# Five of ten neighbourhood value tiles written into the state-space stretch, and attention's first loads written ahead of the rest

## The chip, the cores and the metric

The kernel runs on one core of a Trainium2 chip. The metric is device microseconds of one launch, the median over runs. The core has a tensor engine (PE, with PEld for its weight loads), a vector engine (DVE), a scalar engine (ACT), GpSimd (POOL) and a sync engine (SP), which here issues every transfer. Each takes its own queue of instructions in order; a wait at the head of a queue holds what stands behind it.

## The reference, cut to what matters

Two layers over 1024 latent tokens and 256 context tokens (1280 in all, ten tiles of 128), model width 1024. In each layer one input projection feeds three groups of heads:

```python
na_q, na_k, na_v, df_q, df_k, df_v, s_z, s_xbc, s_dt = jnp.split(h @ w_in, cuts, axis=-1)
y_na = neighbourhood_attention(rms_norm(na_q), rms_norm(na_k), na_v, kc, vc, na_rpb)   # 4 heads of 64
y_df = diff_mixer(df_q, df_k, df_v, ...)     # differential attention: softmax(m0) - lam * softmax(m1)
y_ssm = ssm_mixer(s_z, s_xbc, s_dt, ...)     # bidirectional state-space scan in chunks of 128 tokens
y = jnp.concatenate([y_na, y_df, y_ssm], axis=-1)      # then output projection, residual, gated MLP
```

The change concerns `na_v = h @ w_in[...]` (256 columns, all ten token tiles) and what stands around it. What is computed stays the same.

## The kernel before

All projections work in pairs of high and low parts: an input block or a weight block is split into a rounded part and a remainder, and three matmuls (high by high, high by low, low by high) take the place of one. `load_w` fetches a 128x1024 weight block, copies its high part on ACT (line 268) and subtracts on POOL (line 269). `proj` does 128 output features for chunks of 512, 512 and 256 tokens, three times eight matmuls for a chunk (`proj_chunk`, lines 422 to 424). `proj_tm` does a tile of 128 tokens by 256 features, also 24 matmuls (lines 446 to 448), with weights of two blocks.

The mixer of a layer runs in this order. First come the state-space inputs and states. Then `dfproj` does the differential queries, keys and values, and `naqk` the neighbourhood queries and keys, four blocks in all. During `dfproj` and `naqk` the state-space output (`ssd_all`, a generator with 40 steps in layer 0 and 32 in layer 1, four to a chunk of 128 tokens) runs in the background: after every chunk or tile of a projection, `bg_step` adds `SR` to an account and takes one step from the generator for each whole unit in it. `bg_finish` takes what is left. The output of a state-space chunk ends with a normalization and two stores (`ydd<-zt` and `ydd<-y`, line 1049). This is called the state-space stretch here.

At the handover the memory pools of the state-space output (`ts`) and of the neighbourhood queries and keys (`np`) close, a pool `nv` with two buffers for value tiles and the pool `da` of differential attention open. Then `proj_tm` does the ten tiles of the neighbourhood values. Each is copied by ACT (`nv`, line 846) and stored to DRAM (`nvd`, line 847). Now `df_stream`, the generator of differential attention, is the background, with one step per tile. Its first step loads the keys of two heads (`load_k`: `ks`, four transfers, line 727) and the queries of one tile (`load_q`: `qst`, four transfers, line 734), and does scores (line 759). Each step is one unit: scores of a head for 128 queries, and transposes and values of the unit before.

When the values are done, the layer's input `h` is released. In its place opens the pool `tn` for neighbourhood attention (`natt`), which loads windows of the values (`vw`, `vx`), keys (`nk`, `nqd`) and queries (`nqs`), and the mixed stretch begins: steps of differential attention, of `natt` and of a modulation stream (`ada_native`) are written in turns by the numbers in `streams`.

What sets the order on each engine: the code is traced once, and each instruction gets a priority by its place in the code. A list scheduler then plays the program through with estimated durations, and gives an engine that is free the earliest written instruction among those that are ready, a tile's memory included. So an instruction written early goes first only if it is ready, and one written later may go ahead of it. Memory of a closed pool is reused tile by tile. Three PSUM buffers (`mm`) serve the projections.

Of the kernel before, what the change touches and what calls it, by code (L numbers as in the profile page):

```python
# [10 lines left out]
F32 = mybir.dt.float32  # L11
# [15 lines left out]
NF = 22  # L27
NBIG = -1e30
EB = 6
SR = 1.2  # L30
PA = 0
OORD = (6, 7, 4, 5, 2, 3, 0, 1)
HX = 6
# [43 lines left out]
B_NAV = 22  # L77
# [3 lines left out]
def hybrid_kernel(ctx, tc, xin, cc, w_ada, bada, gmf, w_in, w_dt, w_out, w_up, w_dn, vec, cst, rope, nab, out):  # L81
    nc = tc.nc
    V, S, G, PE, SP = nc.vector, nc.scalar, nc.gpsimd, nc.tensor, nc.sync
# [58 lines left out]
    def at_prio(gen, off):  # L142
        while True:
            with prio(off):
                if next(gen, "end") == "end":
                    return
            yield

    def phase(name, side="left"):
        return tc.tile_pool(name=name, bufs=1, side=side, reuse_waits="tile")  # L150
# [3 lines left out]
    bg_rate = [1.0]  # L154
    bg_due = [0.0]

    def bg_step():
        bg_due[0] += bg_rate[0]
        while bg_due[0] >= 1.0:
            bg_due[0] -= 1.0  # L160
            next(bg[0], None)

    def bg_finish():
        for _ in bg[0]:
            pass
# [251 lines left out]
    def proj_chunk(wh, wl, c0, n, evac, order=range(KT)):  # L417
        ps = mmt()
        for i, k in enumerate(order):
            ks = slice(k * 128, (k + 1) * 128)  # L420
            r = hsl(hH, k, c0, n)
            PE.matmul(ps[:, :n], wh[:, ks], r, start=(i == 0), stop=False)  # L422
            PE.matmul(ps[:, :n], wh[:, ks], hsl(hL, k, c0, n), start=False, stop=False)  # L423
            PE.matmul(ps[:, :n], wl[:, ks], r, start=False, stop=(i == KT - 1))  # L424
        evac(ps[:, :n], c0, n)
        bg_step()

    def proj(src, chunks, evac, order=range(KT)):
        wh, wl = load_w(src)
# [8 lines left out]
    def proj_tm(src2, tiles, evac):  # L438
        w2 = [load_w(s) for s in src2]
        for t in tiles:  # L440
            ps = mmt()
            for k in range(KT):
                wh, wl = w2[k // 4]
                ks = slice((k % 4) * 256, (k % 4 + 1) * 256)
                th, tl = hsl(hH, k, t * 128, 128), hsl(hL, k, t * 128, 128)
                PE.matmul(ps[:, :256], th, wh[:, ks], start=(k == 0), stop=False)
                PE.matmul(ps[:, :256], th, wl[:, ks], start=False, stop=False)
                PE.matmul(ps[:, :256], tl, wh[:, ks], start=False, stop=(k == KT - 1))
            evac(ps[:, :256], t)
            bg_step()  # L450

    ud = [dr.tile([8, 128, T], F32, name=f"ud{l}") for l in range(NL)]
    zd = [dr.tile([4, 128, T], F32, name=f"zd{l}") for l in range(NL)]
# [2 lines left out]
    nvd = [dr.tile([T, 256], F32, name=f"nvd{l}") for l in range(NL)]  # L456
# [58 lines left out]
    def mixer(l):  # L515
        full = l == 0
        qchunks = ALLC if full else MAINC
        NT = 10
# [149 lines left out]

        sd = ExitStack()
        bg[0] = ssd_all(l, sd.enter_context(phase(f"ts{l}")), dts, lah.bitcast(F32), ecs, full)  # L670
        bg_rate[0] = SR
        dfproj(l, dfv, qchunks, lam, gq, gnq, sub, lam_init)


        npx = ExitStack()
        np_ = npx.enter_context(phase(f"np_{l}", "right"))

# [23 lines left out]

            proj(w_in[l, (B_NAQ, B_NAK)[iq] + b], ALLC if iq else qchunks, ev)

        for b in range(2):
            naqk(1, b)
            naqk(0, b)

        bg_finish()
        sd.close()
        npx.close()  # L710
        nvx = ExitStack()
        nv_p = nvx.enter_context(phase(f"nv_{l}", "right"))

        p = da.enter_context(phase(f"da_{l}"))

        def df_stream():
# [74 lines left out]
            def values(b, qt):  # L791
# [34 lines left out]
                SP.dma_start(out=ydd[l][2 + b, 0, :, c0:c0 + n], in_=oh.bitcast(F32))  # L826
                SP.dma_start(out=ydd[l][2 + b, 1, :, c0:c0 + n], in_=sq)

            for i in range(len(units) + 1):
                if i < len(units):  # L830
                    scores(*units[i])
                if i > 0:
                    b, qt, hh = units[i - 1]
                    turn(b, qt, hh)
                    if hh:
                        values(b, qt)
                yield
# [1 line left out]
        ksp = [None]  # L839
        dfs = at_prio(df_stream(), PD)  # L840
        bg[0] = dfs
        bg_rate[0] = 1.0

        def evn(ps, t):
            nv = nv_p.tile([128, 256], F32, tag="nv", name="nv", bufs=2)
            S.copy(out=nv, in_=ps)
            SP.dma_start(out=nvd[l][t * 128:(t + 1) * 128, :], in_=nv)

        proj_tm([w_in[l, B_NAV], w_in[l, B_NAV + 1]], range(NT), evn)
        bg[0] = iter(())  # L850
        nvx.close()
        close_h()
# [5 lines left out]
        with phase(f"tn{l}", "right") as p2:  # L858
            nu = 40 if full else 32
            ksp[0] = p2  # L860
            streams = [(dfs, nu - NT), (natt(l, p2, full), nu), (at_prio(ada_native(p2, todo), PA), 4 * len(todo))]
            total = max(n for _, n in streams)
            done = [0] * len(streams)
            for i in range(total + 2):
                if i == int(HI * total):
                    for k in range(HX, KT):
                        for e in range(2):
                            SP.dma_start(out=(hH, hL)[e][k][0].bitcast(F32), in_=ydd[l][k, e, :, 0:512])
                for j, (g, n) in enumerate(streams):
                    while done[j] * total <= i * n and done[j] <= n:  # L870
                        done[j] += 1
                        if next(g, "end") == "end":
                            done[j] = n + 1
            for g, _ in streams:
                for _ in g:
                    pass
# [1004 lines left out]
```

## Time and profile before

| | us |
|---|---|
| median of 3 runs | 3579.18 (3574.5 to 3580.07) |
| the profiled execution | 3568.3 |
| its span, first to last instruction | 3566.3 |
| mean granted TensorE clock | 0.967 |

The profiled execution is one run of its own. Its span is the time from the first to the last instruction, and 2 us lie around it. The granted clock is a share of full speed, 2.4 GHz; 0.50 is the lower of its two levels, 1.2 GHz. In tables by stretches a number of microseconds behind an engine is its busy time in that stretch, and the number in brackets counts its instructions.

### The profile page before, as it was taken

The page shows a single profiled execution, that of the slowest core. Times are in us where ns is not written, and L with a number is a line of the kernel's source. Part 1 is how long each engine was busy: PE and PEld are TensorE (multiplying, and loading weights), DVE is VectorE, ACT ScalarE, POOL GpSimd, SP SyncE. Part 2 cuts the span into 40 slices and gives each one's busy share as a digit, 9 for nine tenths or more (in the row PEclk, how much of TensorE's full clock was granted, in tenths as well). Part 3 has the DMA queues.
Part 4 walks back from the last instruction along what each step waited for, and adds up shares of the span by engine and source line. Part 5 has one row for each costly group of instructions (what it writes and reads, how often), then busy time and mean ns, then how long its engine had stood idle before and what let it go on. Part 6 is the DMA issues. An engine that isn't in the chain of part 4 may idle for free. (4 is left out here: it accounts for less than half of the span.)

```text
span 3566.3 us, 50227 instructions
## 1 busy us (share of the span) xinstructions
PE 3274.8 (92%) x17970; PEld 2579.0 (72%) x17970; DVE 2272.8 (64%) x4074; ACT 1514.2 (42%) x2641; POOL 1797.8 (50%) x1391
## 2 busy tenths in 40 slices
PE   7998998899888999998998998998998979999899
PEld 3876776667767887887786876776766757777677
DVE  6635875667485555556768745884674666776753
ACT  4233433778263233333335433344774533333343
POOL 2136663667244444544554226663674455555444
PEclk8999999999999999999999999998999989999999
DMA  8355444753722222225443245447555422222633
GB/s 294 105 189 180 133 124 134 193 153 107 260 90 68 89 91 79 89 86 183 145 133 110 84 145 198 125 131 190 169 172 194 152 71 89 92 93 99 240 114 118
DMA packets 328473, 491.24 MB, mean 138 GB/s; under 512 B 28320, under 2 KB 182048, under 8 KB 327968
## 3 DMA queue, kind: packets, MB, share of 16 engines
q1 hardware_dynamic: 328224, 488.03, 43.0%
q8 instruction: 142, 2.33, 0.3%
q14 instruction: 107, 0.88, 0.1%
HBM read 349.25 MB, written 138.67 MB: 137 GB/s over the span
## 5 line engine op out<-in xcount | busy, mean ns | idle before, releaser
L269 POOL TENSOR_TENSOR wL<-wr,wH 128x1024 fp32r<-128x1024 f32 x80 | 204.3, 2557 | 425.9 <-ACT wH L268 384.9
L1226 POOL TENSOR_TENSOR wL<-wr,wH 128x1024 fp32r<-128x1024 f32 (+1 forms) x102 | 229.5, 2252 | 339.5 <-ACT wH L1223 308.5
L760 DVE TENSOR_SCALAR_CACHE_REDUCE e<-s 128x512 f32<-128x512 f32 (+1 forms) x400 | 229.4, 590 | 140.9 <-PE s L759 135.6
L1226 POOL TENSOR_TENSOR wL<-wd,wH 128x512 fp32r<-128x512 f32 (+1 forms) x134 | 215.2, 1623 | 201.0 <-ACT wH L1223 200.6
L1226 POOL TENSOR_TENSOR wL<-ws,wH 128x512 fp32r<-128x512 f32 x168 | 254.1, 1532 | 111.8 <-ACT wH L1223 111.7
L1226 DVE TENSOR_TENSOR bL<-br,bH 128x512 fp32r<-128x512 f32 x154 | 145.4, 948 | 132.0 <-ACT bH L1223 131.0
L93 ACT ACTIVATE e<-e,nm 128x1280 f32<-128x1280 f32 (+1 forms) x144 | 183.3, 1273 | 41.6 <-DVE nm L763 34.4
L1223 ACT CAST wH<-wr 128x1024 fp32r<-128x1024 f32 (+1 forms) x102 | 91.8, 905 | 252.7 <-PE mm L1218 184.0
L1223 ACT CAST wH<-ws 128x512 fp32r<-128x512 f32 x168 | 98.0, 619 | 232.6 <-PE mm L1218 104.1
L772 POOL TENSOR_TENSOR e<-e 128x1280 f32<-128x1280 f32 (+1 forms) x72 | 193.0, 2682 | 3.9
L759 PE MATMUL s<-ks,qst 128*128 128x512 f32 (+1 forms) x400 | 164.5, 449 | 27.9 <-DMA qst<-qkd 13.9
L995 POOL TENSOR_SCALAR mf<-cs,lah 128x128 fp32r<-128x128 f32 x288 | 138.8, 498 | 51.6 <-PE s L997 50.9
L1373 DVE SCALAR_TENSOR_TENSOR fa<-fpad,vc,fa 128x1282 f32<-128x1282 f32 (+1 forms) x88 | 140.6, 1654 | 36.5 <-ACT fa L93 36.5
L1218 PE MATMUL A<-bL,wH 128*128 128x512 f32 x352 | 141.0, 400 | 12.0 <-DVE bL L1226 11.7
L1223 ACT CAST bH<-br 128x512 fp32r<-128x512 f32 x154 | 95.3, 619 | 125.5 <-DMA br<-hdd 55.6
L1223 ACT CAST wH<-wd 128x512 fp32r<-128x512 f32 (+1 forms) x134 | 86.7, 683 | 139.6 <-PE B L1218 70.3
L422 PE MATMUL mm<-h_0H,wH 128*128 128x512 f32 x320 | 135.0, 423 | 4.4 <-DVE aqs L690 3.1
L1219 PE MATMUL A<-bH,wL 128*128 128x512 f32 x352 | 137.6, 397 | 0.0
L423 PE MATMUL mm<-h_0L,wH 128*128 128x512 f32 x320 | 131.5, 411 | 1.9 <-DVE h_0L L402 1.9
L422 PE MATMUL mm<-h_1H,wH 128*128 128x512 f32 x320 | 131.4, 412 | 1.5 <-ACT z L93 1.5
L424 PE MATMUL mm<-h_1H,wL 128*128 128x512 f32 x320 | 130.3, 407 | 0.0
L424 PE MATMUL mm<-h_0H,wL 128*128 128x512 f32 x320 | 130.0, 406 | 0.0
(871 smaller groups left out, 10652.4 us busy)
## 6 DMA issues: line engine op xcount, KB each, us to landing
wr<-in_w_up_dram SPq DMA_DIRECT2D x94, 512.0 KB
br<-hdd SPq DMA_DIRECT2D x154, 256.0 KB
wa<-in_w_ada_dram SPq DMA_DIRECT2D x56, 512.0 KB
wr<-in_w_in_dram SPq DMA_DIRECT2D x48, 512.0 KB
hdd<-c SPq DMA_DIRECT2D x88, 256.0 KB
wr<-in_w_ada_dram SPq DMA_DIRECT2D x40, 512.0 KB
wd<-in_w_dn_dram SPq DMA_DIRECT2D x38, 512.0 KB
hdd<-fa SPq DMA_DIRECT2D x66, 256.0 KB
```

What stands on the lines that cost most here:

```text
L93: ins = S.activation(**kw)
L269: (eng or G).tensor_tensor(out=wl, in0=wr, in1=wh.bitcast(F32), op=ALU.subtract)
L422: PE.matmul(ps[:, :n], wh[:, ks], r, start=(i == 0), stop=False)
L424: PE.matmul(ps[:, :n], wl[:, ks], r, start=False, stop=(i == KT - 1))
L759: PE.matmul(s_, qst[b, qt][:, mi], ks[b][:, mi, k0 + c:k0 + c + n], start=True, stop=True)
L760: V.tensor_scalar(out=e[:, c:c + n], in0=s_, scalar1=1.0, scalar2=None, op0=ALU.mult, op1=ALU.max, accum_out=mx[:, ci:ci + 1])
L772: G.tensor_tensor(out=es[0][:, 0:nk], in0=es[0][:, 0:nk], in1=es[1][:, 0:nk], op=ALU.add)
L995: (V if hh % 2 else G).tensor_scalar(out=mf[:, hh], in0=C(mk), scalar1=lah[:, e, c, h:h + 1], scalar2=1.0, op0=ALU.mult, op1=ALU.mult)
L1218: PE.matmul(ps, wh, bl, start=False, stop=False, skip_group_check=True)
L1223: S.copy(out=out_h, in_=src)
L1226: le.tensor_tensor(out=out_l, in0=src, in1=out_h.bitcast(F32), op=ALU.subtract)
L1373: V.scalar_tensor_tensor(out=a[:, :W], in0=pads[r][:, j:j + W], scalar=vcol(l, fw + j), in1=a[:, :W], op0=ALU.mult, op1=ALU.add)
```

## The change

The first five value tiles are written between the first and the second block of neighbourhood queries and keys, inside the state-space stretch. The other five stay at the handover, so the value weights are loaded by two calls. The pool `nv` opens before `np`. The background's steps are weighted by the columns of the chunk or tile just done (512 columns are 1, a value tile 0.5), and `SR` is 1.5 in layer 0 and 1.3 in layer 1 instead of 1.2. `df_stream` gets a first step of its own with the keys and two tiles of queries, and it is taken before the value tiles of the handover; scores follow from the third tile on. So 3 instead of 10 of its units are written among the value tiles, and the rest goes into the mixed stretch.

```diff
-SR = 1.2
+SR = (1.5, 1.3)
...
-    def bg_step():
-        bg_due[0] += bg_rate[0]
+    def bg_step(w=1.0):
+        bg_due[0] += bg_rate[0] * w
...
(proj_chunk)
-        bg_step()
+        bg_step(n / 512)
...
(proj_tm)
-            bg_step()
+            bg_step(0.5)
...
-        bg_rate[0] = SR
+        bg_rate[0] = SR[l]
         dfproj(l, dfv, qchunks, lam, gq, gnq, sub, lam_init)
+        nvx = ExitStack()
+        nv_p = nvx.enter_context(phase(f"nv_{l}", "right"))
         npx = ExitStack()
         np_ = npx.enter_context(phase(f"np_{l}", "right"))
...
-        for b in range(2):
-            naqk(1, b)
-            naqk(0, b)
-
+        def evn(ps, t):
+            nv = nv_p.tile([128, 256], F32, tag="nv", name="nv", bufs=2)
+            S.copy(out=nv, in_=ps)
+            SP.dma_start(out=nvd[l][t * 128:(t + 1) * 128, :], in_=nv)
+
+        w_nav = [w_in[l, B_NAV], w_in[l, B_NAV + 1]]
+        naqk(1, 0)
+        proj_tm(w_nav, range(5), evn)
+        naqk(0, 0)
+        naqk(1, 1)
+        naqk(0, 1)
         bg_finish()
         sd.close()
         npx.close()
-        nvx = ExitStack()
-        nv_p = nvx.enter_context(phase(f"nv_{l}", "right"))
...
(df_stream)
+            load_k(0)
+            load_q(0, 0)
+            load_q(0, 1)
+            yield
             for i in range(len(units) + 1):
...
         bg[0] = dfs
-        bg_rate[0] = 1.0
-
-        def evn(ps, t):
-            nv = nv_p.tile([128, 256], F32, tag="nv", name="nv", bufs=2)
-            S.copy(out=nv, in_=ps)
-            SP.dma_start(out=nvd[l][t * 128:(t + 1) * 128, :], in_=nv)
-
-        proj_tm([w_in[l, B_NAV], w_in[l, B_NAV + 1]], range(NT), evn)
+        bg_rate[0] = 2.0
+        bg_due[0] = -2.0
+        next(dfs)
+        proj_tm(w_nav, range(5, NT), evn)
...
-            streams = [(dfs, nu - NT), (natt(l, p2, full), nu), (at_prio(ada_native(p2, todo), PA), 4 * len(todo))]
+            streams = [(dfs, nu - 2), (natt(l, p2, full), nu), (at_prio(ada_native(p2, todo), PA), 4 * len(todo))]
```

## Rows read from the trace of the kernel before

**Rows 1.** The page: busy time, share and instructions of each engine.
```profile
PE 3274.8 (92%) x17970; PEld 2579.0 (72%) x17970; DVE 2272.8 (64%) x4074; ACT 1514.2 (42%) x2641; POOL 1797.8 (50%) x1391
```

**Rows 2.** Table by stretches: length, engines' busy time, clock, DMA share, GB/s.
```profile
487.00:572.00 85.00, 80.15 (x435) 59.32 (x435) 75.97 (x148) 35.75 (x73) 55.96 (x69) 0.96 0.40 123
572.00:590.00 18.00, 11.56 (x83) 10.43 (x82) 9.16 (x20) 6.50 (x16) 4.83 (x5) 0.91 0.55 167
590.00:606.00 16.00, 9.48 (x77) 8.88 (x75) 0.00 (x0) 1.02 (x3) 0.00 (x0) 0.93 1.02 227
606.00:647.00 41.00, 33.01 (x210) 27.01 (x210) 21.56 (x84) 21.70 (x38) 22.89 (x15) 0.87 0.43 114
...
2308.00:2404.00 96.00, 92.86 (x510) 73.24 (x509) 80.67 (x160) 39.80 (x79) 67.73 (x84) 0.98 0.41 127
2404.00:2428.60 24.60, 21.77 (x174) 18.71 (x173) 12.84 (x26) 10.83 (x22) 6.59 (x7) 1.00 0.55 170
2428.60:2445.20 16.60, 12.24 (x106) 12.07 (x105) 0.00 (x0) 0.74 (x2) 0.00 (x0) 0.95 0.92 198
2445.20:2473.40 28.20, 23.17 (x108) 15.70 (x108) 19.57 (x76) 19.18 (x31) 18.15 (x12) 0.73 0.52 144
...
2520.00:2700.00 180.00, 173.95 (x1527) 127.03 (x1526) 125.59 (x521) 137.50 (x276) 127.74 (x94) 0.99 0.52 155
```

**Rows 3.** Timeline of SP's queue: start, duration, line, what, count.
```profile
588.70 0.37 SPq L1049 DMA_DIRECT2D ydd<-y  x1
...
589.81 0.39 SPq L727 DMA_DIRECT2D ks<-qkd  x1
...
606.81 12.24 SPq L847 DMA_DIRECT2D nvd<-nv  x6
...
2426.31 0.37 SPq L1049 DMA_DIRECT2D ydd<-y  x1
2428.24 0.32 SPq L847 DMA_DIRECT2D nvd<-nv  x1
2428.66 2.06 SPq L727 DMA_DIRECT2D ks<-qkd  x4
...
2444.29 3.15 SPq L847 DMA_DIRECT2D nvd<-nv  x4
```

**Rows 4.** Timeline of PE: first scores of differential and of neighbourhood attention.
```profile
606.10 1.19 PE L759 MATMUL s<-ks,qst 128*128 128x512 f32 x2 [6.40 <-DMA qst<-qkd]
...
647.30 0.98 PE L1127 MATMUL ns<-nk,nqs 128*128 128x384 f32 x2 [5.35 <-DMA nk<-nqd]
...
2445.19 1.19 PE L759 MATMUL s<-ks,qst 128*128 128x512 f32 x2 [4.36 <-DMA qst<-qkd]
...
2473.36 0.59 PE L1127 MATMUL ns<-nk,nqs 128*128 128x384 f32 x2 [2.91 <-DMA nk<-nqd]
```

**Rows 5.** Table by stretches, PE's instructions of line 446 alone.
```profile
572.00:590.00 18.00, 7.21 (x23) 0.91 0.55 167
590.00:606.00 16.00, 7.18 (x25) 0.93 1.02 227
606.00:647.00 41.00, 9.76 (x32) 0.87 0.43 114
2404.00:2428.60 24.60, 12.73 (x43) 1.00 0.55 170
2428.60:2445.20 16.60, 9.77 (x35) 0.95 0.92 198
```

**Rows 6.** Timeline of ACT: the first copies of value tiles, layer 0.
```profile
590.10 0.65 ACT L846 COPY nv<-mm 128x256 f32<-128x256 f32 x2 [2.25 <-DMA nqd<-aoh]
```

**Rows 7.** Line 269 in 320 to 590: count, shortest, median and longest, ns.
```profile
L269 POOL TENSOR_TENSOR wL<-wr,wH x8: 2345/2364/2689, 336.1 to 546.5; 128x1024 fp32r<-128x1024 f32 x8
```

**Rows 8.** DMA issues of 2428.6 to 2445.2: count, KB each.
```profile
ks<-qkd SPq DMA_DIRECT2D x4, 640.0 KB
qst<-qkd SPq DMA_DIRECT2D x8, 64.0 KB
```

## Prediction

> **What bounds the kernel now.** I read the page first: PE (the tensor engine) is busy 92% of the span, more than any other engine [rows 1], so the change is worth the PE time that it loses or wins. Next the table by stretches [rows 2], cut at the events that the change touches: the neighbourhood query and key projections (487 to 572 us in layer 0, 2308 to 2404 in layer 1), a drain in which the state-space chain runs out (572 to 590, 2404 to 2428.6), the load of attention's keys (590 to 606, 2428.6 to 2445.2) and differential attention alone (606 to 647, 2445.2 to 2473.4). The reader is to see PE busy and granted clock together. I call a stretch minus busy times clock its lost PE time, since at half clock the same work takes twice as long. Layer 0: 85 - 80.15 x 0.96 = 8.1; 18 - 11.56 x 0.91 = 7.5; 16 - 9.48 x 0.93 = 7.2; 41 - 33.01 x 0.87 = 12.3. Layer 1: 96 - 92.86 x 0.98 = 5.0; 24.6 - 21.77 = 2.8; 16.6 - 12.24 x 0.95 = 5.0; 28.2 - 23.17 x 0.73 = 11.3. The mixed stretch of attention behind them loses little (173.95 busy of 180).
>
> Then SP's queue in order of time [rows 3]: the keys `ks` are issued at 589.81 and 2428.66, 1.1 and 2.4 us after the last state-space output `ydd<-y`. In layer 1 the store of a value tile that stands later in the code than `ks` is ahead of it, at 2428.24: so it is not its place in the code that held `ks` back; it became available when the state-space stretch ended. Last the waits of PE [rows 4]: the first score matmul comes at 606.10 and 2445.19, 16.3 and 16.5 us after `ks`, the first neighbourhood score at 647.30 and 2473.36.
>
> **The change part by part.** *Moved matmuls.* A value tile is 24 matmuls, eight on line 446, which counts tiles [rows 5]: 35/8 = 4.4 tiles stand in the key load of layer 1, where PE is busy 12.24 us with them: 2.8 us each. Five tiles are 14.0 us per layer. They enter the projection stretch and leave the handover, which as PE time is plus 14.0 and minus 14.0, sum 0. What counts is the lost PE time that they fill where they arrive, and the loss that they no longer cover where they leave.
>
> *Where they arrive.* The loss is 8.1 and 5.0. The tiles are ready work with only a copy of 0.33 us on ACT behind each [rows 6]. But PE is busy 94 and 97% there and takes its queue in order, so a tile fills only a gap that the plan foresaw. Ends: nothing and all; nearer nothing, for these are waits into which the plan put none of the work it had: -2 and -1.5.
>
> *The repeated weight load.* The projection is called twice, so two blocks are loaded and split twice in each layer: 2 x 2.36 us on POOL [rows 7], a copy on ACT and a load each. POOL is idle 29 of the 85 us, ACT 49, the DMA share is 0.40 [rows 2]: 0, and without that cover 4.7 us per layer, PE standing for both splits.
>
> *Drain and key load together.* Both must pass before a score: the drain because `ks` becomes available at its end, the load for its bytes. It moves 4 x 640 KB of keys and, for the first scores, 4 x 64 KB of queries [rows 8]; the DMA share is 1.02 at 227 GB/s and 0.92 at 198 [rows 2]. It is full already, and putting `ks` and two `qst` ahead of everything saves at most the value store between two `ks` of layer 0, under 1 us: 0. So the length stays, 34 and 41.2 us, and PE can use it only with what work it has. Layer 0 now has (23 + 25)/8 = 6.0 tiles there, layer 1 (43 + 35)/8 = 9.8 [rows 5]; after the change there are five. The copy of a value tile no longer waits for memory of the projections (the first now comes at 590.10, after the last of them [rows 6]), so the five will run in the drain and none stands over the load. Layer 0: 1.0 x 2.8 = +2.8. Layer 1: 4.8 x 2.8 = +13.4. Ends 0 and 14.0 each. In place of PE's wait of 6.4 and 4.4 us before the first score [rows 4] I expect some 15.
>
> The Trainium skill has a rule that speaks against this, "DMA: Bandwidth & Descriptors", Rules for kernel authors, "Overlap DMA with compute": issue the load early, compute, and wait late. Taken alone it would charge every moved tile as lost cover, 28 us for both layers; by the rows above it is 16.2, since layer 0 does four tiles only after the load.
>
> *Differential attention alone.* What is late next are the neighbourhood loads: they need the memory of the layer's input, which the last value tile frees, and SP issues them behind `qst`. In layer 0 the six value stores from 606.81 on, 12.2 us [rows 3], and waits around them go, so the first neighbourhood score comes some 15 us sooner after `ks` (42.5 instead of 57.5); in layer 1 the four stores from 2444.29 on, 3.2 us (41.5 instead of 44.7). Without the 4.0 tiles of layer 0 (32 on line 446) the same scores in 26 us lose 26 - (33.01 x 0.87 - 4.0 x 2.8) = 8.5, so -3.8; layer 1, with next to no tile there, 25.0 - 23.17 x 0.73 = 8.1, so -3.2. Ends 0 and -12.3, -11.3. About seven score units move from here into the mixed stretch, where ACT is busy 137.5 of 180 us, less than PE: +1 per layer (ends 0 and +4).
>
> *The pace.* State-space steps (40 and 32) are now taken by columns. The last one falls in layer 0 one chunk earlier than before (40/1.5 = 26.7 of 27.5; 33.3 of 34 calls), in layer 1 in the last chunk instead of three before the end (32/1.3 = 24.6 of 25.5; 26.7 of 30). A later step can lengthen layer 1's drain, with no tile left for it: +1 (ends -3 and +8; three chunks are at most five tiles' columns, 14 us, of which the chain already lags). Layer 0: 0 (ends -7.5 and +3, one tile ahead of the chain's matmul in PE's queue).
>
> Sum, layer 0: -2 + 0 + 2.8 - 3.8 + 1 + 0 = -2.0. Layer 1: -1.5 + 0 + 13.4 - 3.2 + 1 + 1 = +10.7. Together +9 on the profiled execution's 3568.3 us (a span of 3566.3 and 2 around it). The median of the three runs, 3579.18, stands 10.9 above that execution; the 9 go on the median: 3588.
>
> **The rivals.** *The drain closes (faster).* If the evener pace lets the state-space chain end with the projections, `ks` comes that much sooner and the five tiles stand over the load after all. For: drains of 18 and 24.6 us are a chain of short waits, DVE busy only 9.16 and 12.84 [rows 2]. Against: in layer 1 the last step was already written three chunks before the end of the projections, and the chain still ended 22 us after them. Ten us shorter in each layer gives 9 - 20 = -11, 3568. It decides from 9 us in both together; from 16 the kernel is measurably faster.
>
> *The stretch takes the tiles for nothing (no change).* All of the 8.1 and 5.0 is filled, 9.6 more than I took: about 0, 3579. For: the clock there is 0.96 and 0.98, so waits cost twice, and filler would keep it up. Against: PE busy 94 and 97%. The Trainium skill, "Perfetto Trace Analysis", Optimization Strategy, recommends interleaving regimes whose most-contended engines differ, and by it this would be the main effect. The rows bear it out in part only: PE is the busiest engine on both sides.
>
> *Worse than forecast.* In layer 1 the clock is 0.73 over 2445 to 2473, after a wait of 4.4 us; with 15 us of wait layer 0 may do the same: 33.01 x (0.87 - 0.73) = 4.6, and with layer 1's later chain at +8 instead of +1: 9 + 12 = 21, 3600. It is the upper part of the forecast's case.
>
> *`ks` really comes sooner (faster).* Up to 16 us a layer would be at stake, 3579 + 9 - 32 = 3556, if its place in the code held it. Layer 1's store ahead of it speaks against [rows 3]: 0.04.
>
> **How the numbers follow.** A measurement of this kernel can tell about 0.2% from no change, 7.2 us. The forecast with its upper part has 0.43, its own range 3583 to 3602, and 0.03 of it lies within 0.2%; the stretch filled has 0.27, the drain closed 0.26, sooner keys 0.04. So slower 0.40, same 0.30, faster 0.30. The range for 8 in 10 takes in the closed drain with some 5 us of the unknown ends below it, 3563, and the upper part with the 4.7 us of one late weight load above it, 3605, rounded to 3606.
>
> **What would show it.** Right: the copies of tiles five to nine all ahead of `ks` in both layers; PE idle some 15 us before the first score, which stays 16 after `ks`; the first neighbourhood score 42 us after `ks`; projection stretches about 12 us longer. Wrong: the last `ydd<-y` close behind the last projection matmul; value matmuls between `ks` and the first score; `ks` ahead of the last state-space output; projection stretches grown by under 8 us.

## Result and the profile after

| | before | after |
|---|---|---|
| median | 3578.93 us (4 runs, 3574.50 to 3580.07) | 3598.86 us (4 runs, 3595.94 to 3606.97) |
| ratio | | 1.0063 [1.0042, 1.0084] |
| profiled execution, its span, clock | see above | 3601.38, 3599.5, 0.957 |

The change makes the kernel 19.9 us slower by the medians (by the interval, 15 to 30). Slower was forecast, but by 9 us. The profiled executions differ by 33, because that of before was 10.6 below the median of its runs and that of the change 2.5 above.

The page of the changed kernel: PE's busy time has hardly moved from [rows 1], the span is 33 us longer.

```profile
PE 3275.2 (91%) x17970; PEld 2581.0 (72%) x17970; DVE 2294.6 (64%) x4074; ACT 1520.0 (42%) x2645; POOL 1792.2 (50%) x1395
```

SP's queue around the keys in the changed kernel, layer 0 and then layer 1; it answers to [rows 3].

```profile
608.33 0.39 SPq L1056 DMA_DIRECT2D ydd<-y  x1
...
610.89 0.32 SPq L702 DMA_DIRECT2D nqd<-aqsq  x1
...
612.28 1.05 SPq L734 DMA_DIRECT2D ks<-qkd  x2
...
2451.49 0.32 SPq L702 DMA_DIRECT2D nqd<-aqsq  x1
...
2455.51 0.54 SPq L1056 DMA_DIRECT2D ydd<-y  x1
...
2457.79 2.29 SPq L734 DMA_DIRECT2D ks<-qkd  x4
```

Two things end the state-space stretch: the last scan output `ydd<-y` and the last store of the neighbourhood queries and keys, `nqd<-aqsq`. The keys `ks` follow the later of the two by 1.4 and 2.3 us. In layer 0 that is the neighbourhood store. It was so before the change too, though [rows 3] show the scan's store alone:

```profile
589.39 0.32 SPq L700 DMA_DIRECT2D nqd<-aqsq  x1
```

ACT's last copies of value tiles in layer 0, then PE's first scores, which answer to [rows 4].

```profile
610.32 0.37 ACT L708 COPY nv<-mm 128x256 f32<-128x256 f32 x1 [0.31 <-PE mm L448]
613.16 0.37 ACT L708 COPY nv<-mm 128x256 f32<-128x256 f32 x1 [2.47 <-PE mm L448]
```

```profile
628.42 1.19 PE L766 MATMUL s<-ks,qst 128*128 128x512 f32 x2 [15.35 <-DMA qst<-qkd]
...
652.42 0.98 PE L1134 MATMUL ns<-nk,nqs 128*128 128x384 f32 x2 [7.68 <-DMA nk<-nqd]
...
2474.00 1.19 PE L766 MATMUL s<-ks,qst 128*128 128x512 f32 x2 [19.49 <-DMA qst<-qkd]
...
2493.90 0.98 PE L1134 MATMUL ns<-nk,nqs 128*128 128x384 f32 x2 [8.88 <-DMA nk<-nqd]
```

In layer 0 the tenth tile is copied 0.9 us after `ks` was issued, all the others before it; in layer 1 all ten are copied before it, the last at 2454.55. PE then waits 15.35 and 19.49 us for its first score (6.40 and 4.36 before).

The table by stretches after the change, columns as in [rows 2]: for layer 0 the end of the state-space stretch, then for each layer the key load, differential attention alone, and the mixed stretch up to the output projection's first matmul on `T20H`. That matmul is taken as the end of the mixed stretch because its input is loaded behind the last store of differential attention; six matmuls of the output projection on other blocks run earlier.

```profile
592.00:612.28 20.28, 17.94 (x135) 16.80 (x132) 12.96 (x24) 9.40 (x21) 4.79 (x4) 0.92 0.59 184
612.28:628.42 16.14, 0.80 (x7) 0.62 (x7) 0.00 (x0) 0.37 (x1) 0.00 (x0) 0.64 0.99 212
628.42:652.42 24.00, 14.53 (x33) 7.92 (x34) 13.18 (x50) 10.27 (x15) 9.13 (x6) 0.57 0.58 149
652.42:936.64 284.22, 256.86 (x2194) 191.20 (x2194) 189.60 (x788) 208.06 (x454) 191.95 (x163) 0.94 0.51 143
...
2457.79:2474.00 16.21, 0.00 (x1) 0.03 (x1) 0.00 (x0) 0.00 (x0) 0.00 (x0) 0.50 1.00 215
2474.00:2493.90 19.90, 9.26 (x16) 4.24 (x16) 9.63 (x37) 7.28 (x10) 9.11 (x6) 0.50 0.52 130
2493.90:2765.07 271.17, 246.97 (x2155) 183.16 (x2155) 174.79 (x707) 191.19 (x381) 174.72 (x129) 0.95 0.54 155
```

The same mixed stretches in the kernel before:

```profile
647.30:919.77 272.47, 250.47 (x2112) 183.88 (x2112) 180.10 (x754) 199.95 (x438) 179.50 (x154) 0.94 0.54 152
2473.36:2733.57 260.21, 241.63 (x2072) 176.60 (x2072) 162.06 (x668) 180.94 (x363) 167.29 (x124) 0.96 0.56 161
```

Neighbourhood attention does start 17.2 and 8.3 us sooner after the first score (24.0 and 19.9 us instead of 41.2 and 28.2). But in those shorter stretches less of attention's work is done: DVE is busy 13.18 and 9.63 us there, where [rows 2] have 21.56 and 19.57, and POOL 9.13 and 9.11 instead of 22.89 and 18.15. The mixed stretch behind grows by 11.8 and 11.0 us, and its end shows who is late. SP's stores at the end of layer 0's mixed stretch, first before the change, then after it: `doh` and `dsq` are outputs of differential attention, `nyh` and `nyl` of neighbourhood attention.

```profile
912.30 0.32 SPq L827 DMA_DIRECT2D ydd<-dsq  x1
913.29 0.32 SPq L1186 DMA_DIRECT2D ydd<-nyh  x1
913.70 0.38 SPq L1187 DMA_DIRECT2D ydd<-nyl  x1
```

```profile
918.04 0.38 SPq L1194 DMA_DIRECT2D ydd<-nyl  x1
...
933.48 0.32 SPq L834 DMA_DIRECT2D ydd<-dsq  x1
933.89 0.38 SPq L1676 DMA_DIRECT2D T20H<-ydd  x1
```

Before, both kinds of attention end within 1.4 us of each other (5.1 in layer 1). After, neighbourhood attention is done 15.4 us ahead (18.1 in layer 1), and the last units of differential attention run alone but for the first six matmuls of the output projection. PE in that end, after the change:

```profile
921.95 0.66 PE L808 MATMUL o<-at,dfv 128*64 128x128 f32 x8 [2.44 <-DVE dsq L831]
...
926.48 1.22 PE L824 MATMUL t<-dsq,cs 128*128 128x256 f32 x2 [2.50 <-ACT dsq L93]
927.63 1.12 PE L827 MATMUL t<-cs,dg 128*64 128x128 f32 x8
936.64 0.79 PE L422 MATMUL mm<-T20H,wH 128*128 128x512 f32 x1 [7.88 <-DMA T20H<-ydd]
```

From its first score to its last store differential attention took 306.2 and 285.1 us before and 305.1 and 287.8 after, although four tiles less stand beside it in layer 0. What it starts later, it ends later.

### The profile page after: what moved, and what is told of

It is laid out like the page before. It is cut to its first block, busy times and chain, and to the rows that moved or that the text cites. A ratio compares the mean times of both kernels' runs of the same rounds, so it can differ in the third digit from the quotient of the medians.

```text
span 3599.5 us, 50246 instructions
## 1 busy us (share of the span) xinstructions
PE 3275.2 (91%) x17970; PEld 2581.0 (72%) x17970; DVE 2294.6 (64%) x4074; ACT 1520.0 (42%) x2645; POOL 1792.2 (50%) x1395
## 5 line engine op out<-in xcount | busy, mean ns | idle before, releaser
L269 POOL TENSOR_TENSOR wL<-wr,wH 128x1024 fp32r<-128x1024 f32 x84 | 212.8, 2536 | 414.9 <-ACT wH L268 353.1
L1233 POOL TENSOR_TENSOR wL<-wr,wH 128x1024 fp32r<-128x1024 f32 (+1 forms) x102 | 227.0, 2227 | 334.7 <-ACT wH L1230 325.5
L1225 PE MATMUL A<-bL,wH 128*128 128x512 f32 x352 | 141.6, 402 | 12.0 <-DVE bL L1233 11.8
L766 PEld LDWEIGHTS s<-ks,qst 128*128 128x128 f32 x400 | 76.2, 205 | 99.2 <-issue 50.7
L1002 DVE TENSOR_SCALAR mf<-cs,lah 128x128 fp32r<-128x128 f32 x288 | 115.5, 458 | 26.8 <-PE s L1004 26.4
```

The costliest lines, as they stand in the source:

```text
L269: (eng or G).tensor_tensor(out=wl, in0=wr, in1=wh.bitcast(F32), op=ALU.subtract)
L766: PE.matmul(s_, qst[b, qt][:, mi], ks[b][:, mi, k0 + c:k0 + c + n], start=True, stop=True)
L1002: (V if hh % 2 else G).tensor_scalar(out=mf[:, hh], in0=C(mk), scalar1=lah[:, e, c, h:h + 1], scalar2=1.0, op0=ALU.mult, op1=ALU.mult)
L1225: PE.matmul(ps, wh, bl, start=False, stop=False, skip_group_check=True)
L1233: le.tensor_tensor(out=out_l, in0=src, in1=out_h.bitcast(F32), op=ALU.subtract)
```

## The experiments

Every kernel was timed beside the kernel before. The table lists, for layer 0 / layer 1 of the profiled execution: "keys", from the first rotation of the differential queries (`t<-qn,cs`, 306.21 and 2173.94 us before) to `ks`; "wait", PE's wait just ahead of the first score; "rest", from the first score to the output projection's first matmul on `T20H`. One row is one execution.

| kernel | ratio to before [95%] | keys | wait | rest |
|---|---|---|---|---|
| before | | 283.6 / 254.7 | 6.4 / 4.4 | 313.7 / 288.4 |
| the change | 1.0063 [1.0042, 1.0084] | 307.7 / 263.5 | 15.4 / 19.5 | 308.2 / 291.1 |
| e1 old pace | 1.0071 [1.0059, 1.0083] | 297.5 / 267.7 | 14.7 / 15.6 | 306.6 / 298.3 |
| e2 pace alone | 1.0023 [1.0014, 1.0032] | 303.7 / 253.3 | 8.9 / 3.5 | 314.8 / 281.0 |
| e3 loads first alone | 0.9988 [0.9973, 1.0002] | 292.9 / 256.7 | 9.6 / 4.3 | 318.1 / 285.6 |
| e4 tiles alone | 1.0101 [1.0086, 1.0116] | 303.1 / 273.5 | 14.6 / 15.1 | 313.1 / 294.5 |
| e8 none moved | 1.0075 [1.0053, 1.0097] | 307.8 / 256.9 | 15.1 / 9.0 | 310.0 / 301.2 |
| e9 useless cover | 1.0130 [1.0108, 1.0152] | 305.7 / 265.1 | 3.8 / 7.6 | 317.2 / 300.9 |
| e11 late buffers | 1.0094 [1.0073, 1.0115] | 303.2 / 261.7 | 7.5 / 10.6 | 314.7 / 296.8 |
| e10 units ahead | 1.0077 [1.0060, 1.0094] | 304.4 / 264.8 | 15.3 / 20.4 | 311.3 / 290.2 |
| e13 ten units | 1.0067 [1.0051, 1.0084] | 307.4 / 264.0 | 16.0 / 20.0 | 311.7 / 293.2 |
| e7 half keys, after | 1.0033 [1.0020, 1.0047] | 304.6 / 264.8 | 9.3 / 13.7 | 302.4 / 296.4 |
| e6 half keys, before | 0.9987 [0.9973, 1.0001] | 290.1 / 253.5 | 1.6 / 3.6 | 325.5 / 281.8 |
| e12 both, before | 0.9991 [0.9978, 1.0005] | 283.3 / 256.6 | 3.3 / 4.2 | 318.7 / 295.2 |

In layer 0 e3, e6 and e12 issue PE's instructions in the same order as the kernel before up to the handover, and e7, e9, e10 and e13 in that of the change, but for a handful of matmuls. So "keys" can be averaged: 287.5 over four (283.3 to 292.9) against 306.0 over five (304.4 to 307.7) in layer 0. In layer 1, where no edit between them touches the stretch, it is 255.4 (253.5 to 256.7) against 264.4 (263.5 to 265.1). The keys come 18.5 and 9.0 us later.

**The change taken apart.** First theory: two causes, the cover over the key load and new gaps by the pace.

e1, the change with the old pace:

```diff
-SR = (1.5, 1.3)
+SR = (1.2, 1.2)
-        bg_step(n / 512)
+        bg_step()
-            bg_step(0.5)
+            bg_step()
-        bg_rate[0] = 2.0
+        bg_rate[0] = 1.0
```

> The change without its pacing edit: 1.2 steps for every chunk or tile again, whatever its columns, one step per tile at the handover. Tiles moved and loads first stay. Theory A (two causes: the moved tiles are gone as cover over the key load, some 12 us in both layers together, and the new pace opens gaps in layer 0's differential projections, some 8 us): 3591, that is 8 faster than the change; the PE time lost between 320 and 480 us in layer 0 back from 23 to about 14; the first score still 16 us after the keys, PE still waiting over 13 us before it. Theory B (the pace is the whole loss, the tiles move for nothing): 3579, and the wait before the first score costs nothing because the stretch ahead of it is shorter by as much. Theory C (loading attention's first keys and queries ahead of the tiles is the loss): 3599 as with the whole change.

It measured 27.2 us slower than before, no better than the change. Theory C fits the total, A's 8 us back did not come. The pace moved time between the layers: the keys come 10 us sooner in layer 0 and 4 later in layer 1 than in the change.

e2, the kernel before with the new pace:

```diff
-SR = 1.2
+SR = (1.5, 1.3)
-        bg_step()
+        bg_step(n / 512)
-            bg_step()
+            bg_step(0.5)
-        bg_rate[0] = 1.0
+        bg_rate[0] = 2.0
+        bg_due[0] = 0.0
```

> The kernel before with the pacing edit alone: steps by columns, 1.5 in layer 0 and 1.3 in layer 1; at the handover still one step per tile. All ten value tiles stay at the handover, no loads-first step. Theory A: 3587, 8 slower than before, all of it in layer 0's differential projections (lost PE time between 320 and 480 us 23 instead of 14), with the handover as before: value tiles over the key load, PE waiting 4 to 7 us before the first score. Theory B: 3599. Theory C: 3579.

8.5 us slower, as A said, but for another reason than the gaps it named. PE does lose 160 - 148.56 x 0.93 = 21.8 us between 320 and 480 us, where the kernel before lost 160 - 149.07 x 0.98 = 13.9; but e3, which has the old pace and the order of the kernel before, loses 160 - 147.50 x 0.92 = 24.3 there. So such gaps come without the new pace too. SP's queue in e2, layer 0:

```profile
593.88 0.69 SPq L700 DMA_DIRECT2D nqd<-aqsq  x1
...
608.94 0.39 SPq L1050 DMA_DIRECT2D ydd<-y  x1
609.42 1.00 SPq L727 DMA_DIRECT2D ks<-qkd  x2
```

The last scan output comes 15.1 us behind the last neighbourhood store; before it was 0.7 ahead of it (588.70 in [rows 3], the store at 589.39). By columns, the ten differential value tiles get 0.75 steps each instead of 1.2, so 4.5 steps fewer, and four steps are one chunk of the scan. The trace fits: the fifth chunk's output, which falls there, comes at 476.76 us in e2, against 461.73 before and 470.84 in e3, and the scan does not make it up (its last output comes at 608.94, against 588.70 and 596.83). No run changed the value tiles' steps alone. In e1, with the old pace and the tiles, it is the other way round:

```profile
587.48 0.53 SPq L1056 DMA_DIRECT2D ydd<-y  x1
...
601.16 0.32 SPq L702 DMA_DIRECT2D nqd<-aqsq  x1
...
602.97 1.40 SPq L734 DMA_DIRECT2D ks<-qkd  x3
```

The scan ends 13.7 us before the projections. Each of the two edits alone makes one of the two ends late; together they are level again (608.33 and 610.89), some 18 us later than before.

e3, the kernel before with the loads first:

```diff
+            load_k(0)
+            load_q(0, 0)
+            load_q(0, 1)
+            yield
...
+        next(dfs)
         proj_tm([w_in[l, B_NAV], w_in[l, B_NAV + 1]], range(NT), evn)
```

> The kernel before with one edit: attention's first keys and two tiles of queries are written as a step of their own ahead of the ten value tiles. Theory A: nothing, 3579 within 4 us, since the keys become ready only when the state-space chain ends; keys at about 590 and 2429 us, first score 16 us behind. Theory C: 3590 to 3599, with the keys' load bunched so that tiles or stores behind it come later. If the keys' place in the code had held them, they would come sooner and the kernel be faster, 3570 or less.

5.1 us faster by the medians, an interval that includes no change: nothing or little, as A said. `ks` still follows the last neighbourhood store by 0.4 us (597.52 and 597.93), so its place in the code had not held it.

e4, the tiles alone: the change with the old pace of e1 and without the loads-first step (`nu - 5` units in the mixed stretch).

```diff
-SR = (1.5, 1.3)
+SR = (1.2, 1.2)
-            load_k(0)
-            load_q(0, 0)
-            load_q(0, 1)
-            yield
-        bg_rate[0] = 2.0
-        bg_due[0] = -2.0
-        next(dfs)
+        bg_rate[0] = 1.0
```

> Of the change only the five value tiles, moved with their two weight blocks into the state-space stretch; old pace (1.2 per chunk or tile, a value tile counting as a full step), no loads-first step. Theory A: 3591 (12 slower than before), PE waiting over 13 us before the first score in both layers, the clock at 0.5 to 0.65 just behind that wait, and no new gaps between 320 and 480 us. Theory B: 3579. Theory C: 3579. A fourth outcome, under 3572, would mean that the tiles fill waits of the state-space stretch and that the rest of the change spoils it.

36.3 us slower, three times A's 12. The tiles alone cost more than the whole change, and the rest of the change makes that smaller. With the old pace (e1 and e4) the keys come at 300.3 and 270.6 on average, 12.8 and 15.2 us later than before: about the 14 us of the tiles themselves, with little or nothing of it filled into gaps.

e8, the change without the moved tiles:

```diff
-        proj_tm(w_nav, range(5), evn)
...
-        proj_tm(w_nav, range(5, NT), evn)
+        proj_tm(w_nav, range(NT), evn)
-            streams = [(dfs, nu - 2), ...
+            streams = [(dfs, nu - 7), ...
```

> The change without its moved tiles: all ten value tiles at the handover, but the new pace and attention's loads first (seven more units of attention stay in the handover, as it now has ten tiles' worth of steps). Theory A (the moved tiles are the loss, and the pace and the loads first only change its size): 3581, the 8 that the pace cost alone less the 4 of loads first; PE's wait before the first score 9 us at most. Theory B (the new pace with the loads first is the loss, and the tiles add only what they showed without them): 3595 or more.

27.8 us slower, with no tile moved: theory A falls, and putting the tiles back into the handover wins nothing over the change (1.0075 against 1.0063). The late scan of the new pace alone puts layer 0's keys as late as in the change (307.8), and nine of the ten tiles, whose buffers are free early here, run ahead of the keys. Layer 1's first score is only 1.7 us later than before, but its rest is 301.2, 20 us longer than in e2. So this kernel loses time that no later first score explains. What makes that so is open: e8 differs from e2 in the early pool `nv`, in the loads first and in seven units instead of ten in the handover.

**Is the wait the price?** Second theory: the time is lost in PE's wait and in the half clock behind it.

e9, useless work in the wait:

```diff
-        proj_tm(w_nav, range(5, NT), evn)
+        wh, wl = proj_tm(w_nav, range(5, NT), evn)[0]
+        ps = mmt()
+        for _ in range(96):
+            PE.matmul(ps[:, :256], wh[:, 0:128], wl[:, 0:256], start=True, stop=True)
```

> The change plus 96 matmuls of 128x128 by 128x256 behind the last value tile in each layer, on the value weights' own tiles, into a buffer that nobody reads: 11 us of work at full clock that has no use, in PE's wait before the first score. Theory A (after a wait of 15 to 19 us attention's first matmuls run at half clock, which costs some 9 us in layer 0 and 5 in layer 1): 3587, the first score at the same distance of 16 us from the keys, the granted clock behind it near 1 instead of 0.5, and the first neighbourhood scores sooner. Theory B (the clock costs nothing there, because attention alone waits for its loads and for the vector engine anyway): 3599. Theory C (work in the wait only delays the scores): 3605 or more.

45.6 us slower than before. PE in the wait of layer 0, and the table by stretches for the key load and differential attention alone:

```profile
611.24 11.43 PE L860 MATMUL mm<-wL,wH 128*128 128x256 f32 x94
626.47 1.19 PE L767 MATMUL s<-ks,qst 128*128 128x512 f32 x2 [3.79 <-DMA qst<-qkd]
```

```profile
609.95:626.47 16.52, 12.73 (x108) 12.55 (x106) 0.00 (x0) 0.37 (x1) 0.00 (x0) 0.97 0.95 209
626.47:650.27 23.80, 14.86 (x34) 8.30 (x34) 12.80 (x48) 10.28 (x15) 9.13 (x6) 0.57 0.58 149
```

The clock over the key load is 0.97 and PE is at work up to 3.8 us before the first score, yet behind it the clock is 0.57, as in the change. So the length of the wait is not what puts attention's first 24 us near half clock, and A's outcome did not come. But e9 does not show what a wait costs, because it leaves 3.8 us of it (7.6 in layer 1). In e6, described below, PE idles 1.57 us before the first score in layer 0 and 3.62 in layer 1; the stretches just behind:

```profile
604.57:608.00 3.43, 3.43 (x27) 3.34 (x28) 1.31 (x4) 0.38 (x1) 0.00 (x0) 1.00 1.02 215
...
2452.12:2456.00 3.88, 3.88 (x18) 3.69 (x19) 1.31 (x4) 0.00 (x0) 0.00 (x0) 0.56 1.07 223
```

Full clock is granted behind the one and near half behind the other. No run has scores alone behind no wait at all, so what the half clock costs stays open. The total of e9 is C's and worse: the first score came no later in layer 0 and 1.6 us later in layer 1, but the mixed stretch became 9.2 and 9.9 us longer than in the change. Why is open.

e11, the last five tiles in late buffers, so that real work stands in the wait:

```diff
-        nvx = ExitStack()
-        nv_p = nvx.enter_context(phase(f"nv_{l}", "right"))
         npx = ExitStack()
         np_ = npx.enter_context(phase(f"np_{l}", "right"))
+        nvx = ExitStack()
+        nv_p = nvx.enter_context(phase(f"nv_{l}", "right"))
...
         sd.close()
+        nvx.close()
         npx.close()
+        nvx = ExitStack()
+        nv_p = nvx.enter_context(phase(f"nw_{l}", "right"))
```

> The change with the five tiles of the handover in buffers that lie, as in the kernel before, in memory of the neighbourhood queries and keys, so that their copies can only begin when that memory is free; the first five keep buffers of their own. Theory A (the two PSUM-deep tiles ahead aside, the five then stand over the key load instead of in the drain, and that cover is what the change lost): PE's wait before the first score 3 to 6 us instead of 15 and 19, and 3580 to 3585. Theory B (drain and key load are one hole of fixed length, and it does not matter where in it the five stand): the wait shorter, but the state-space stretch loses as much more, 3595 to 3602.

32.8 us slower. The key loads of both layers:

```profile
608.10:623.95 15.85, 8.38 (x66) 8.21 (x66) 0.00 (x0) 0.65 (x2) 0.00 (x0) 0.82 0.96 205
2463.06:2479.05 15.99, 5.37 (x46) 5.19 (x46) 0.00 (x0) 0.74 (x2) 0.00 (x0) 0.82 1.02 220
```

PE's wait is half as long, and the kernel is no faster than the change: the total is B's and rather more. Some 66/24 = 2.8 and 46/24 = 1.9 tiles, 7.7 and 5.4 us, now stand behind the keys, but the keys come only 2.8 and 2.7 us sooner than the averages of the change's order, and the rest is not shorter (314.7 and 296.8). Drain and key load are nearly one hole; where in it the tiles stand won nothing. The Trainium skill, "DMA: Bandwidth & Descriptors", Rules for kernel authors, "Overlap DMA with compute", says to issue a load early, compute, and wait late. In e11 real work under the load did not pay: what the end waited for did not come sooner by it.

**What follows the first score.** Third theory: differential attention sets the end, or else the end of the mixed stretch does.

e10, differential attention ahead:

```diff
-PD = 0
+PD = -1000
-            streams = [(dfs, nu - 2), (natt(l, p2, full), nu), ...
+            streams = [(dfs, nu + 4), (natt(l, p2, full), nu - 8), ...
```

> The change with differential attention ahead in the mixed stretch: its units get a priority 1000 places earlier and are written in more turns (counts nu + 4, against nu - 8 of neighbourhood attention), so that neighbourhood attention ends the stretch, as it does in the kernel before. In the change its last store comes 15 and 18 us ahead of that of differential attention, and in the last 20 us before the output projection 15 and 11 us of PE time are lost, against 9 and 5 before. Theory A (these 6 us a layer are part of the loss, the price of the units that left the handover): tails of 9 and 5 again, 3583 to 3589. Theory B (differential attention takes some 305 and 288 us from its first score whatever stands beside it, so the order at the end does not matter): 3595 or more, the tail lost elsewhere.

28.1 us slower, theory B. Layer 1, the second pair's keys in SP's queue, then differential attention alone and the last 20 us:

```profile
2480.74 2.13 SPq L734 DMA_DIRECT2D ks<-qkd  x4
```

```profile
2481.47:2513.60 32.13, 13.35 (x32) 7.39 (x32) 12.04 (x46) 10.27 (x15) 9.13 (x6) 0.55 0.72 163
...
2751.70:2771.70 20.00, 14.98 (x134) 11.04 (x134) 3.96 (x10) 7.46 (x18) 4.89 (x4) 1.00 0.32 103
```

The tail is mended in layer 1: 20 - 14.98 = 5.0 us lost, where the change loses 20 - 8.74 x 0.80 = 13.0 (the expectation's 11 is that sum in slices of 5 us). But the stretch ahead is 12.2 us longer, with the second pair's keys issued ahead of the neighbourhood loads (`vw` from 2482.92 on), and the layer's rest is 290.2 us as in the change (291.1). In layer 0 the tail is mended in part: neighbourhood attention ends 6.9 us ahead instead of 15.4, and the last 20 us lose 20 - 11.06 x 0.77 = 11.5 us instead of 20 - 6.73 x 0.68 = 15.4. The rest there is no shorter either (311.3 and 308.2).

e13, ten units in the handover again:

```diff
-        bg_rate[0] = 2.0
-        bg_due[0] = -2.0
+        bg_rate[0] = 4.0
+        bg_due[0] = 0.0
-            streams = [(dfs, nu - 2), ...
+            streams = [(dfs, nu - 9), ...
```

> The change with ten instead of three units of differential attention written among the value tiles of the handover (four steps for every 512 columns, from the first tile on; the count in the mixed stretch nu - 9 instead of nu - 2), so that seven units a layer stand ahead of neighbourhood attention again, as in the kernel before. Up to the first score nothing differs. Theory A (the units that left the handover for the mixed stretch cost some 10 us in layer 1, where the kernels with nine or more units in the handover take 281 to 295 us from the first score to the output projection and those with fewer 290 to 301): 3587 to 3591, layer 1 from first score to output projection under 288. Theory B (which units are written where changes nothing, the layer's loss is the later first score): 3597 to 3602, 291 us there as in the change.

24.7 us slower, theory B, with 293.2 us of rest in layer 1: how many units are written in the handover made no difference here.

e7, the change with the keys in two tiles:

```diff
-            def load_k(b):
-                t = (p if b == 0 else ksp[0]).tile([128, 4, T], F32R, tag="ks", name="ks")
+            def load_k(b, hh):
+                t = (p if b == 0 else ksp[0]).tile([128, 2, T], F32R, tag=f"ks{hh}", name="ks")
...
-            load_k(0)
+            load_k(0, 0)
             load_q(0, 0)
+            load_k(0, 1)
             load_q(0, 1)
```

> The change with the keys in two tiles, one for each head of the pair: the first head's 1.28 MB, then the queries, then the second head's keys. Theory A (the wait before the first score is the length of the load that it needs, and each us of it is paid): the first score 9 us after the keys instead of 16, 3583 to 3587. Theory B (what follows waits for the whole of the transfers anyway, the second head's keys and the neighbourhood loads behind them): first score sooner, neighbourhood scores not, 3597 to 3601.

12.2 us slower than before, so 0.30% or 10.7 us better than the change (2 to 20 by the two intervals). The first score in e7, both layers, with `ks` at 610.13 and 2445.68:

```profile
620.20 1.19 PE L766 MATMUL s<-ks,qst 128*128 128x512 f32 x2 [9.29 <-DMA qst<-qkd]
...
2456.09 1.19 PE L766 MATMUL s<-ks,qst 128*128 128x512 f32 x2 [13.67 <-DMA ks<-qkd]
```

It comes 10.1 and 10.4 us after the keys instead of 16.1 and 16.2, together 11.8 sooner, which is near the 10.7 that the medians give. By layers the two do not match: from the rotation to the end of the rest the profiled execution takes 15.1 us less than the change in layer 0 and 0.7 more in layer 1, whose rest is 5.3 us longer. This is the only edit on the changed kernel that won anything, and the only one that shortened the load that the first score waits for.

e6, the same edit on the kernel before (there with the keys loaded by the first score, as before):

> The kernel before with the keys in two tiles in the same way. Value tiles stand over the load there, and PE waits only 6.4 and 4.4 us before the first score. Theory A: these waits go, 3568 to 3572. Theory B: the value tiles and the scores change places and PE waits as long elsewhere, 3577.

4.6 us faster, an interval that just includes no change: between the theories. The first scores come 6.5 and 4.6 us sooner after the keys, but in layer 0 the neighbourhood scores do not (45.6 us after the first score instead of 41.2), and there both kinds of attention end nearly together.

e12, the half keys of e6 and the loads first of e3 together, on the kernel before:

```diff
+            load_k(0, 0)
+            load_q(0, 0)
+            load_k(0, 1)
+            load_q(0, 1)
+            yield
...
+        next(dfs)
```

> The kernel before with the keys in two tiles, and attention's first transfers (first head's keys, a tile of queries, second head's keys, a tile of queries) written ahead of the ten value tiles. No tile is moved, the pace is the old one. Alone, each of the two edits measured 4 to 5 us faster than the kernel before, neither beyond doubt. Theory A (they act on different waits and add): 3567 to 3569 where before is 3577, a ratio of 0.9975. Theory B (both only shift the order by chance): a ratio between 0.9985 and 1.0015.

3.6 us faster, not told from no change: theory B. No version was found that surely beats the kernel before.

## Why the prediction was right, and where its sum was not

**Direction and range held.** The forecast was 3588 (3563 to 3606). The handover became what it described: nine and ten tiles copied ahead of `ks`, a wait of 15.35 and 19.49 us where "some 15" stood, a first score 16.1 and 16.2 us after the keys, neighbourhood scores 40.1 and 36.1 us after them (42 forecast). The size did not: 9 is under half of the 19.9 measured.

**What comes before the first score: right in sum, with some luck.** The terms give +12 in layer 0 (14.0 - 2 with a fixed length of drain and load) and +13.5 in layer 1, 25.5 together. Averaged, the keys came 18.5 and 9.0 later, 27.5. The layers are off by +6.5 and -4.5, which nearly cancel.

**The pace, layer 0 "0", is mis-sized.** With the old pace the tiles cost 12.8 there (e1, e4), with the new one 18.5: +5.7. I looked where the last step falls, not at the 4.5 steps that the differential value tiles lost. In layer 1 it was not +1 but 9.0 - 15.2 = -6.2. The two nearly cancel; by the total, e1 and the change do not differ. In layer 0 tiles and pace do not add: the pace alone makes the keys 16.2 late (e2, 303.7 less 287.5), and with it the moved tiles add hardly anything (e8, 307.8 with none moved). The later of two ends counts there.

**The stretch's gaps, -2 and -1.5.** With the pace unchanged 12.8 and 15.2 us came for 14.0 us of tiles: -1.2 and +1.2, small as forecast. The rival in which the stretch takes the tiles for nothing is out.

**The drain in layer 0 was misread.** I took it for the scan alone. Before, scan and neighbourhood stores end 0.7 us apart, so a sooner scan by itself would have freed nothing. The rival of the closing drain did half happen: in the change the scan ends 2.6 us ahead of the projections. But it is the projections that came later.

**The repeated weight load, 0.** It shows as four more instructions on POOL and on ACT (1395 and 2645 instead of 1391 and 2641). No run prices it alone.

**What comes back after the first score is the term that failed.** In layer 0 the sum took off 11.2 us for 4.0 tiles that no longer stand there and 3.8 for differential attention alone, and added 1: -14.0. In layer 1 it was -0.6, -3.2 and +1: -2.8. Together -16.8. Averaged over the kernels of equal key loads (the change, e10, e13 against before, e3), the rest went from 315.9 to 310.4 and from 287.0 to 291.5: -5.5 and +4.5, together -1.0. The term "differential attention alone", -3.8 and -3.2, was mis-sized. The PE time lost there, which I had put at 8.5 and 8.1, was 24.0 - 14.53 x 0.57 = 15.7 and 19.9 - 9.26 x 0.50 = 15.3; against 12.3 and 11.3 before that is +3.4 and +4.0. With these the rest would be -6.8 and +4.4, close to what was measured. The premise that failed is "the same scores" in a stretch 15 and 3 us shorter: less of them was done in it (DVE busy 13.18 instead of 21.56 us, 9.63 instead of 19.57), and what was left over lengthened the mixed stretch. Neighbourhood attention's sooner start won nothing by itself, since differential attention now ends last by 15.4 and 18.1 us.

**The sum as measured:** +27.5 up to the keys, +0.2 from keys to first score, -1.0 behind it: 26.7 by averaged stretches, beside 19.9 (15 to 30) by the runs of the change and 24.7 by those of e13.

**What is shown and what is not.** Shown: up to the first score the loss is the keys' delay, 27.5 us by averages of five executions against four; behind it the rest did not get shorter to make up for it. That holds across the experiments too: in the fourteen executions, both layers together, a straight line through the times gives an end 0.98 us later for each us by which the first scores come later. Single executions lie up to 12.6 us off that line, e9 farthest, and the loss of e8 in layer 1 and of e9 behind the first score is not explained by it. Also shown: the written order of units behind the first score did not matter (e10, e13), and real work under the key load did not pay (e11). Not shown: that the moved tiles are the one cause. With the old pace they delay the keys by their own length (e1, e4), but with the new pace, the loads first and the early pool the kernel is as slow without them (e8). Argued only: that differential attention's length is a chain of its own. It was 303 to 316 us in layer 0 (299 in e7) and 278 to 298 in layer 1, whatever stood beside it; PE is some nine tenths busy in it, and I did not find what sets it. The worse rival's 3600 was near in size with one of its two terms: the clock behind the first score of layer 0 did fall, to 0.57 where it put 0.73, but the later chain in layer 1 did not come (9.0 us for 14.0 of tiles), and what the clock costs there is open.

## What to carry to other kernels

Ask of moved filler first whether it delays the start of the longest stream behind it: ahead of differential attention the tiles cost about their full length, while the rest became only 5.5 us shorter when four of them, 11.2 us, no longer stood beside it. Idle time in a wait need not be the price; putting real work into it won nothing here (e11), a shorter load won 10.7 us (e7). When a stretch gets shorter, do not assume that a chain inside it does the same work in less time. Where two chains end a stretch level, weigh an edit on both, and follow a paced background through every kind of foreground work, not only to its last step.

## Unexpected

The granted clock behind the first score was 0.57 in layer 0 both after 15 us of idle PE and after 11.4 us of matmuls that ended 3.8 us before it; in layer 1 of e9 it was 0.50 as in the change. The same PE order up to the handover took 283.3 to 292.9 us in layer 0 in four executions, so a stretch of one execution is good to some 9 us, half of what this change moved. A good part of that lies in the clock: between 320 and 480 us it was 0.98 in the kernel before and 0.92 in e3, with PE busy 149.07 and 147.50 us.
